# Two layers of a hybrid diffusion backbone: the buffers of the later stages shifted within 512 bytes

## The chip, the core and the metric

The kernel runs on one core of a Trainium2 chip. The core has a matrix engine (TensorE, "PE" in the profile, with its weight loads listed apart as "PEld"), a vector engine (VectorE, "DVE"), a scalar engine (ScalarE, "ACT"), a general engine (GpSimd, "POOL") and a queue engine (SyncE, "SP") that issues most of the transfers. All of them work on one on-chip memory, SBUF, of 128 partitions; matrix products land in a second one, PSUM, of eight banks. An address of a buffer below means its first byte inside each partition.

The metric is device microseconds of one execution. A time is the median of several executions; beside it stands the range. The profile is of one further execution, with its own time.

## The reference

A stream of 512 latent tokens and 256 context tokens, 1,024 wide, passes through two layers. Each sub-layer is norm, modulation, mixer, norm, gate, residual. In outline, with the shapes that matter:

```python
for layer in range(2):
    hl, hc = modulate(rmsnorm(xl), ...), modulate(rmsnorm(xc), ...)
    if layer == 0:
        p = h @ w_in                       # 1024 x 2944: gating MLP + RWKV-7, both directions
        y = concat(spatial_gate(p), rwkv_bidir(p)) @ w_out
    else:
        p = h @ c_w_in                     # 1024 x 2064: mLSTM, 4 heads, both directions
        y = mlstm_out(mlstm_chunk_scan(...)) @ c_w_out
    x = x + gate * rmsnorm(y)
    a, b = split(h @ ffn_up)               # 1024 x 5632
    y = (gelu(depthwise_conv(a)) * b) @ ffn_down      # 2816 x 1024
    x = x + gate * rmsnorm(y)
return xl
```

Layer 1 needs the context tokens only up to the mLSTM's state; its output projection and its ConvFFN run on the 512 latent tokens alone.

## The kernel before

**How a dense product is done.** Everything is kept in float32, and a dense product is made of three products in a reduced format: each operand is split into a rounded part `hi` and a remainder `lo`, and `hi*hi + hi*lo + lo*hi` is accumulated in one PSUM bank. Each contraction step of 128 rows is therefore three matmuls. Such a matmul has a stationary operand of 128 x 128 values (512 bytes in each partition, read by the weight load) and a moving operand of 128 x 512 (latent tokens, or 512 output columns; 2,048 bytes) or 128 x 256 (context tokens). There are two forms:

- `proj_pass` (lines 259 to 270), for `w_in`, `c_in`, the gates and both `ffn_up`: the weight slice is stationary, the transposed tokens `hT` are moving. A pass is 8 contraction steps, 24 matmuls. Names in the profile: `pl_...` for the latent tokens (128x512), `pc_...` for the context (128x256).
- `down` (lines 1033 to 1057), for `w_out`, `c_out` and both `ffn_down`: the tokens are stationary (`a`, `ah`/`al`, or `hhi`/`hlo`), the weight row of 1,024 columns is moving, in halves of 512. Names: `oo` and `of`.

**The stages, in order of time.** Input projections of layer 0 with the preparation of the RWKV scan (to about 380 us of the profiled span), the scan (to 626), `w_out` (to 699), `ffn_up` of layer 0 (to 1075), `ffn_down` of layer 0 (to about 1272), gates, input projections and the mLSTM of layer 1 (to about 1549), `c_out` (to 1584, then the norm), `ffn_up` of layer 1 (1597 to 1843), `ffn_down` of layer 1 (to 1966), the last norm and store.

**What sets the order.** Each engine works through its own list in the order in which the program was written, with generators woven together by hand in the RWKV and mLSTM stages. An instruction waits on semaphores for its operands and for the buffer that it overwrites. In `ffn_up` of layer 0 a filler (`ada_sums`, lines 185 to 205) is woven under the products: five steps for each of the 22 units, all on DVE and POOL.

**Where the buffers lie.** Pools are allocated as two stacks, one from the low end of SBUF upwards, one (`side="right"`) from the high end downwards. A pool begins where the pool under it ends. Tiles inside the pools used by the dense products are multiples of 512 bytes, and the slices that a matmul reads begin at multiples of 512 bytes in them, so all operands of one pool share one offset within 512 bytes. In the built program these are:

| dense product | stationary operand, offset within 512 | moving operand, offset within 512 | matmuls of 128x512 | of 128x256 |
|---|---|---|---|---|
| `w_in` (layer 0 inputs) | weights, right stack: 480 | `hT`, right stack: 480 | 552 | 552 |
| `w_out` | `a`, right stack: 480 | `wo`, left stack: 352 | 288 | 0 |
| `ffn_up`, layer 0 | weights, left stack: 352 | `hT`, right stack: 480 | 1,056 | 1,056 |
| `ffn_down`, layer 0 | `hhi`, `hlo`, left stack, above `fpar`: 224 | weights, left stack: 352 | 792 | 0 |
| gates and `c_in`, layer 1 | weights, left stack: 352 | `hT`, right stack: 480 | 408 | 216 |
| `c_out` | `ah`, `al`, right stack: 480 | `wo`, left stack: 352 | 192 | 0 |
| `ffn_up`, layer 1 | weights, left stack: 352 | `hT`, right stack: 480 | 1,056 | 0 |
| `ffn_down`, layer 1 | `hhi`, `hlo`, left stack: 224 | weights, left stack: 352 | 528 | 0 |

So the input projections of layer 0 have both operands at one offset; in every other dense product they are 128 bytes apart (one way or the other). `fpar`, the table of convolution weights in `ffn`, has 220 values of 4 bytes, 880 bytes, and takes 896 in its pool; the pool `fs`, which holds `hhi` and `hlo`, begins after it.

Of the kernel before, what the change touches and what calls it, by code (L numbers as in the profile page):

```python
# [8 lines left out]
F32 = mybir.dt.float32  # L9
# [5 lines left out]
P = 128  # L15
# [36 lines left out]
PF = _Cols()  # L52
# [17 lines left out]
def build(tc, *args, **kw):  # L70
    with ExitStack() as ctx:
        _build(ctx, tc, *args, **kw)


def _build(ctx, tc, xall, par, cst, ada_0, ada_w, ada_t, w_in, w_out, ffn_up, ffn_down, lora, wsT, a_bs, c_in, c_gate, c_out, mneg, parf, parm, out):
# [983 lines left out]
    def ffn(l, xt, hT, ctx_too, after, final=None, beneath=None):  # L1059

        with ExitStack() as fx:
            hidp = fx.enter_context(tc.tile_pool(name=f"fhid{l}", bufs=1))
            hid = [hidp.tile([P, NH, w], F32, tag=f"hid{g}", name=f"hid{l}{g}") for g, w in ((0, TL), (1, TC))[:2 if ctx_too else 1]]
            fpar = hidp.tile([P, PF.n], F32, name=f"fpar{l}")
            nc.scalar.dma_start(fpar, parf[l])
            sp = fx.enter_context(tc.tile_pool(name=f"fs{l}", bufs=1))
            fill = beneath(sp) if beneath else None
# [71 lines left out]


    strm.sub, strm.hi, strm.lo = nc.vector, 3, 3
    xp = ctx.enter_context(tc.tile_pool(name="x", bufs=1))
    H = {tg: ctx.enter_context(tc.tile_pool(name=f"H{tg}", bufs=1, side="right")) for tg in ("lat", "ctx")}
    xcx = ExitStack()
# [56 lines left out]
    def beneath(pool):  # L1201
# [6 lines left out]
        return ada_sums(rows, place)  # L1208

    ffn(0, xt, hT, True, to_layer1, None, beneath)  # L1210


    xcx.close()
    hT = hT1
    with ExitStack() as ox:
# [280 lines left out]
        with tc.tile_pool(name="op1", bufs=1) as op2:  # L1496
# [9 lines left out]
            hT = h_tiles(H, "h1f", False)  # L1506
            norm_T(1, 1, xt, hT, op2, lambda i: op2.tile([P, D], F32, tag="xin", name=f"xs1{i}", bufs=4), 2, 4, 0, "02461357")
    ffn(1, xt, hT, False, None, out)


# [98 lines left out]
```

## Time and profile before

| | |
|---|---|
| median of 3 executions | 1970.32 us (1968.26 to 1972.65) |
| the profiled execution, its own time | 1975.72 us |
| its span, first to last instruction | 1973.8 us |
| granted TensorE clock, mean over the span | 0.965 |
| PE busy | 1854.0 us, 94% of the span, 12,411 matmuls |
| weight loads busy | 1508.3 us, 76% |
| DVE busy | 1334.4 us, 68% |
| ACT, POOL busy | 800.1 us, 306.9 us |
| moved by DMA | 227.77 MB, mean 115 GB/s |

How to read it. A matmul's row gives its start and a length; the ends are modelled, and matmuls overlap in the array, so that a stream of them has a length of about 0.39 us each and still begins a new one every 0.23 us. What counts for time is the distance from one start to the next. It can be read from the rows in order of time, or from a window in which PE is busy throughout: the window's length over the number of matmuls in it. A window's number in "(x...)" takes in the matmuls that had begun before it and were not over (at 0.39 us of length and 0.23 us of distance, 1.7 of them on the mean). Windows are counted in microseconds from the span's first instruction. Records are to 0.01 us in the rows in order of time.

### The profile page before, as it was taken

The numbers are of one execution on the slowest core, as the hardware profiler recorded it, in microseconds if no ns is written. First come the engines' busy times: TensorE is split into PE (matmuls) and PEld (weight loads), VectorE is DVE, ScalarE is ACT, GpSimd is POOL, SyncE is SP. The second block draws the span as 40 slices with busy tenths as digits, with TensorE's granted clock in tenths as the row PEclk, the third lists the DMA queues.
The fourth block names the chain that finished last, engine by engine and source line by source line (L and its number), as shares of the span: only waits on it lengthen the run. The fifth ranks groups of instructions, "written<-read, shape, count | busy, mean of one in ns | idle before, by whom it ended". The sixth has DMA issues, their size and how long they took to land.

```text
span 1973.8 us, 31872 instructions
## 1 busy us (share of the span) xinstructions
PE 1854.0 (94%) x12411; PEld 1508.3 (76%) x12411; DVE 1334.4 (68%) x2669; ACT 800.1 (41%) x1429; POOL 306.9 (16%) x429
## 2 busy tenths in 40 slices
PE   6998789698898999999999998999999989999998
PEld 4777677587666888888888886778888768888886
DVE  4379675757345589999994337667777688777534
ACT  4364645534335442222222226475554353323222
POOL 2222222311000222223330002100110020000001
PEclk9999889788899999999999999999999999999999
DMA  7133121643764524444432224431111312222222
GB/s 292 54 123 123 57 103 55 182 123 83 204 184 138 182 99 160 150 160 165 161 134 76 97 96 160 151 92 44 33 43 44 139 56 96 96 96 96 88 94 86
DMA packets 102887, 227.77 MB, mean 115 GB/s; under 512 B 28224, under 2 KB 44048, under 8 KB 99664
## 3 DMA queue, kind: packets, MB, share of 16 engines
q1 hardware_dynamic: 100976, 222.26, 33.4%
q10 hardware_dynamic: 1760, 3.47, 0.5%
q8 instruction: 98, 1.61, 0.3%
q14 instruction: 53, 0.43, 0.1%
HBM read 199.31 MB, written 26.39 MB: 114 GB/s over the span
## 4 chain that ended last, share of the span: by engine, by line
PE 58%; DVE 2%; POOL 1%; ACT 1%; issue 1%; DMA 0%; DVEq 0%; SPq 0%; ACTq 0%; POOLq 0%
PE of L1044 5%; PE of L1043 5%; PE of L1045 5%; PE pl_fb L268 4%; PE pl_fb L266 4%; PE pl_fb L267 4%; PE pl_fa L267 4%; PE pl_fa L268 4%; PE pl_fa L266 4%; PE pd L1453 1%; PE pe L1430 1%; PE kv L1386 1%; PE pc_fa L267 1%; PE pc_fa L266 1%; PE pc_fb L266 1%; PE pc_fb L268 1%
## 5 line engine op out<-in xcount | busy, mean ns | idle before, releaser
L1091 DVE SCALAR_TENSOR_TENSOR cv<-pl_fa,fpar,cv 128x441 f32<-128x441 f32 (+2 forms) x352 | 243.1, 691 | 16.5 <-ACT cv L1080 11.3
L1045 PE MATMUL of<-hi_fd,hlo 128*128 128x512 f32 x440 | 173.4, 396 | 3.0 <-DVE hlo L1115 3.0
L1044 PE MATMUL of<-lo_fd,hhi 128*128 128x512 f32 x440 | 174.6, 397 | 1.4 <-DVE lo_fd L125 1.4
L1043 PE MATMUL of<-hi_fd,hhi 128*128 128x512 f32 x440 | 173.7, 397 | 0.0
L201 DVE SCALAR_TENSOR_TENSOR aj<-am,srb 128x512 f32<-128x512 f32 x224 | 163.3, 729 | 10.0 <-DMA am<-in_ada_t_dram 5.6
L1115 DVE TENSOR_TENSOR hlo<-hid,hhi 128x512 fp32r<-128x512 f32 (+1 forms) x66 | 39.2, 601 | 133.9 <-ACT hhi L1114 133.7
L1114 ACT ACTIVATE hhi<-hid 128x512 fp32r<-128x512 f32 (+1 forms) x66 | 36.7, 559 | 177.2 <-PE of L1044 173.5
L1045 PEld LDWEIGHTS of<-hi_fd,hlo 128*128 128x128 f32 x440 | 83.2, 189 | 22.6 <-DVE hlo L1115 3.4
L1044 PEld LDWEIGHTS of<-lo_fd,hhi 128*128 128x128 f32 x440 | 83.3, 189 | 21.5 <-DVE lo_fd L125 2.3
L125 DVE TENSOR_TENSOR lo_fd<-raw_fd,hi_fd 128x1024 fp32r<-128x1024 f32 x66 | 80.8, 1224 | 26.0 <-ACT hi_fd L124 25.8
L1043 PEld LDWEIGHTS of<-hi_fd,hhi 128*128 128x128 f32 x440 | 83.1, 189 | 19.8 <-ACT hi_fd L124 0.5
L222 POOL TENSOR_SCALAR rstd_p_f<-sq_f,sq_f 128x1 f32<-128x1 f32 x10 | 6.9, 689 | 569.6 <-ACT jk_f L1022 569.6
L124 ACT ACTIVATE hi_fd<-raw_fd 128x1024 fp32r<-128x1024 f32 x66 | 69.2, 1049 | 28.7 <-DMA raw_fd<-in_ffn_down_dram 12.2
L124 ACT ACTIVATE hi_fa<-raw_fa 128x1024 fp32r<-128x1024 f32 x44 | 46.4, 1054 | 79.0 <-PE pl_fb L267 64.4
L124 ACT ACTIVATE hi_fb<-raw_fb 128x1024 fp32r<-128x1024 f32 x44 | 46.7, 1061 | 69.6 <-PE pc_fa L267 38.5
L125 POOL TENSOR_TENSOR lo_fb<-raw_fb,hi_fb 128x1024 fp32r<-128x1024 f32 x22 | 59.4, 2699 | 88.8 <-ACT hi_fb L124 88.8
L125 POOL TENSOR_TENSOR lo_win<-raw_win,hi_win 128x1024 fp32r<-128x1024 f32 x23 | 57.5, 2503 | 90.9 <-ACT hi_win L124 90.0
L1093 ACT ACTIVATE cv<-cv 128x512 f32<-128x512 f32 x44 | 27.8, 632 | 106.7 <-DVE cv L1091 106.7
L267 PE MATMUL pl_fa<-h1f_latlo,hi_fa 128*128 128x512 f32 x176 | 69.6, 396 | 0.0
L266 PE MATMUL pl_fb<-h0f_lathi,hi_fb 128*128 128x512 f32 x176 | 69.6, 396 | 0.0
L268 PE MATMUL pl_fa<-h0f_lathi,lo_fa 128*128 128x512 f32 x176 | 69.6, 395 | 0.0
L267 PE MATMUL pl_fb<-h0f_latlo,hi_fb 128*128 128x512 f32 x176 | 69.5, 395 | 0.0
(695 smaller groups left out, 5507.4 us busy)
## 6 DMA issues: line engine op xcount, KB each, us to landing
raw_fd<-in_ffn_down_dram SPq DMA_DIRECT2D x66, 512.0 KB, 3.2
am<-in_ada_t_dram SPq DMA_DIRECT2D x112, 256.0 KB, 3.0
raw_fa<-in_ffn_up_dram SPq DMA_DIRECT2D x44, 512.0 KB, 3.3
raw_fb<-in_ffn_up_dram SPq DMA_DIRECT2D x44, 512.0 KB, 3.2
raw_win<-in_w_in_dram SPq DMA_DIRECT2D x23, 512.0 KB, 3.3
ada<-in_ada_dram SPq DMA_DIRECT2D x8, 1024.0 KB, 8.9
ada<-in_ada_w_dram SPq DMA_DIRECT2D x8, 1024.0 KB, 8.0
raw_cin<-in_c_in_dram SPq DMA_DIRECT2D x16, 512.0 KB, 3.4
```

What stands on the lines that cost most here:

```text
L124: nc.scalar.activation(hi[:, c], raw[:, c], AF.Copy)
L125: strm.sub.tensor_tensor(lo[:, c], raw[:, c], hi[:, c].bitcast(F32), ALU.subtract)
L201: V.scalar_tensor_tensor(place(f"aj{i}{h}{cnd}", "junk"), raw, 1.0, sb[cnd * 2 + h], ALU.mult, ALU.mult, accum_out=acc[:, cnd, h:h + 1])
L266: mm(p, wh[:, kt, :], hh[:, kt], start=(kt == 0), stop=False)
L267: mm(p, wh[:, kt, :], hl[:, kt], start=False, stop=False)
L268: mm(p, wl[:, kt, :], hh[:, kt], start=False, stop=(kt == KT - 1))
L1043: mm(o[i][hf], hi, w[0][:, c], start=f, stop=False)
L1044: mm(o[i][hf], hi, w[1][:, c], start=False, stop=False)
L1045: mm(o[i][hf], lo, w[0][:, c], start=False, stop=e)
L1091: V.scalar_tensor_tensor(dv, src[:, r0 + dy:r1 + dy, c0 + dx:c1 + dx], fw(ky * 3 + kx), dv, ALU.mult, ALU.add)
L1114: A.activation(hi, hid[cnd][:, k], AF.Copy)
L1115: V.tensor_tensor(lo, hid[cnd][:, k], hi.bitcast(F32), ALU.subtract)
```

## The change

Two edits, neither of which touches a computation. A tile of 32 values (128 bytes) named `gap`, which nothing writes or reads, is put on the left stack ahead of the pool `x`. And `fpar` is allocated with 256 values (1,024 bytes) in place of 220; its first 220 are used as before.

```diff
@@ ffn @@
             hidp = fx.enter_context(tc.tile_pool(name=f"fhid{l}", bufs=1))
             hid = [hidp.tile([P, NH, w], F32, ...) for g, w in ((0, TL), (1, TC))[:2 if ctx_too else 1]]
-            fpar = hidp.tile([P, PF.n], F32, name=f"fpar{l}")
+            fpar = hidp.tile([P, 256], F32, name=f"fpar{l}")[:, :PF.n]
             nc.scalar.dma_start(fpar, parf[l])
             sp = fx.enter_context(tc.tile_pool(name=f"fs{l}", bufs=1))
@@ after layer 0's scan @@
     strm.sub, strm.hi, strm.lo = nc.vector, 3, 3
+
+    ctx.enter_context(tc.tile_pool(name="gap", bufs=1)).tile([P, 32], F32, name="gap")
     xp = ctx.enter_context(tc.tile_pool(name="x", bufs=1))
```

In the built program every engine has the same instructions in the same order with the same waits as before; the line numbers after the second edit are two higher. What differs is addresses on the left stack. The pools from `x` upwards (`x`, `xc`, the weight pools `strm` and `strmr`, `wo`, `op0`, `op1`, `wk1` and the others) begin 128 bytes later, at an offset of 480 within 512 where they had 352. The pools `fs0` and `fs1` begin 256 bytes later, at 480 where they had 224. The right stack and everything before `w_out` stay where they were. With that, both operands of every dense product in the table above lie at offset 480. Operands that were not part of a dense product move along: the transposes of the norms and of the mLSTM output (160 in all) now have their two operands 160 or 256 bytes apart where it was 288 or 384; the state products of the mLSTM (`pd`, `pe`) keep their distances, since both operands lie in the same moved pools.

## Prediction

> **What bounds the kernel now.** I read the page first (busy shares, the chain that ended last), then the busy time of each engine by stage, then the rows of single matmuls.
>
> ```profile
> PE 1854.0 (94%) x12411; PEld 1508.3 (76%) x12411; DVE 1334.4 (68%) x2669; ACT 800.1 (41%) x1429; POOL 306.9 (16%) x429
> ...
> PE 58%; DVE 2%; POOL 1%; ACT 1%; issue 1%; DMA 0%; DVEq 0%; SPq 0%; ACTq 0%; POOLq 0%
> ```
>
> PE is busy nearly throughout and carries the chain; no other engine has more than 2% of it. The stages, by windows (columns: length, then busy time and count for PE, weight loads, DVE, ACT, POOL, then PE clock, DMA share, GB/s):
>
> ```profile
> 626.00:699.00 73.00, 70.82 (x320) 57.23 (x320) 44.30 (x74) 38.40 (x77) 13.80 (x19) 1.00 0.52 178
> 699.00:1075.00 376.00, 373.97 (x2130) 325.43 (x2129) 341.71 (x770) 104.09 (x153) 100.68 (x139) 1.00 0.41 142
> 1075.00:1175.00 100.00, 100.00 (x435) 80.76 (x434) 35.25 (x43) 27.96 (x35) 0.00 (x0) 1.00 0.28 98
> 1175.00:1285.00 110.00, 100.68 (x432) 79.47 (x430) 70.30 (x104) 58.42 (x109) 19.30 (x24) 0.95 0.43 151
> 1340.00:1504.00 164.00, 162.72 (x907) 136.04 (x906) 123.03 (x334) 82.52 (x177) 15.01 (x38) 1.00 0.16 46
> 1504.00:1597.00 93.00, 83.23 (x417) 66.10 (x416) 62.57 (x145) 39.25 (x89) 16.39 (x30) 0.96 0.24 85
> 1597.00:1843.00 246.00, 246.00 (x1059) 198.98 (x1058) 192.41 (x256) 81.25 (x98) 0.00 (x0) 1.00 0.26 93
> 1843.00:1966.00 123.00, 122.87 (x529) 99.28 (x527) 46.06 (x53) 36.47 (x54) 3.90 (x6) 1.00 0.24 83
> ```
>
> In both `ffn_up`, both `ffn_down` and `w_out` PE has no idle time to speak of at full clock, so there the time is the number of matmuls times the distance between their starts. The nearest other engine is DVE in `ffn_up` of layer 0, 341.71 of 376 us.
>
> **The price of one matmul, at two placements.** The kernel before has both: `w_in` with its operands at one offset, the rest 128 bytes apart. First the rest, in windows that are all dense matmuls of 128x512 (`ffn_up` of layer 1, `ffn_down` of layer 1 and of layer 0, `w_out`). The first two rows have all engines' columns, the others PE alone; the first is the pass of `w_in` that comes after:
>
> ```profile
> 79.05:84.51 5.46, 5.46 (x26) 4.51 (x25) 2.58 (x1) 1.33 (x2) 2.39 (x1) 1.00 0.13 41
> 1600.00:1840.00 240.00, 240.00 (x1035) 194.53 (x1034) 186.65 (x246) 79.39 (x94) 0.00 (x0) 1.00 0.26 93
> ...
> 1845.00:1965.00 120.00, 120.00 (x518) 1.00 0.24 84
> 1080.00:1195.00 115.00, 115.00 (x496) 1.00 0.28 98
> 632.00:672.00 40.00, 40.00 (x174) 1.00 0.68 230
> ```
>
> With 1.7 taken off each count for those begun before: 240/1033.3 = 232.3 ns, 120/516.3 = 232.4, 115/494.3 = 232.7, 40/172.3 = 232.2. One price, whichever operand lies on which stack, and whether DMA runs at 84 or 230 GB/s and DVE is 37% or 78% busy (46.06 of 123, 186.65 of 240). Now the pass of `w_in`, at the same clock of 1.00, in rows of time (start, length), 24 latent matmuls and then the context ones:
>
> ```profile
> 79.05 0.40 PE L266 MATMUL pl_kT<-h_lathi,hi_win 128*128 128x512 f32 x1
> ...
> 80.43 0.39 PE L266 MATMUL pl_kT<-h_lathi,hi_win 128*128 128x512 f32 x1
> ...
> 83.83 0.39 PE L266 MATMUL pl_kT<-h_lathi,hi_win 128*128 128x512 f32 x1
> ...
> 84.51 0.28 PE L266 MATMUL pc_kT<-h_ctxhi,hi_win 128*128 128x256 f32 x1
> ...
> 87.27 0.28 PE L268 MATMUL pc_kT<-h_ctxhi,lo_win 128*128 128x256 f32 x1
> ```
>
> From 80.43 to 83.83 lie 15 distances: 3.40/15 = 226.7 ns. The first six of the pass are longer, 1.38/6 = 230.0; the pass with its step into the next is 5.46/24 = 227.5. In the pass the distance between the two operands' addresses changes by 1,536 bytes at each contraction step, and the price stays 226.7: only the place within 512 bytes is the same throughout. The context matmuls, 24 starts: (87.27 - 84.51)/23 = 120.0. Their like in `ffn_up` of layer 0, 128 bytes apart:
>
> ```profile
> 903.62 0.28 PE L266 MATMUL pc_fb<-h0f_ctxhi,hi_fb 128*128 128x256 f32 x1
> ...
> 906.35 0.28 PE L268 MATMUL pc_fb<-h0f_ctxhi,lo_fb 128*128 128x256 f32 x1
> ...
> 906.92 0.40 PE L268 MATMUL pl_fa<-h0f_lathi,lo_fa 128*128 128x512 f32 x1
> 907.17 0.40 PE L266 MATMUL pl_fa<-h0f_lathi,hi_fa 128*128 128x512 f32 x1
> ...
> 908.55 0.40 PE L266 MATMUL pl_fa<-h0f_lathi,hi_fa 128*128 128x512 f32 x1
> 908.79 0.40 PE L267 MATMUL pl_fa<-h0f_latlo,hi_fa 128*128 128x512 f32 x1
> ```
>
> 2.73/23 = 118.7. So one offset makes the wide matmul 5.6 ns shorter once it has settled (232.3 - 226.7), 4.8 in passes of 24 between narrow ones (232.3 - 227.5), and the narrow one 1.3 ns longer (the rows' 0.01 us leave about 0.6 on that). The last four rows show how the 128 bytes cost: one long distance (907.17 - 906.92 = 0.25) and the next long one 7 starts later (908.79 - 908.55 = 0.24); the seven from 906.92 to 908.55 are 1.63/7 = 232.9. The slowness turns up in a cycle, as if two reads drift past each other; at one offset they lock, and stay at the short distance.
>
> [...]
>
> **The change part by part.** Nothing is added to any engine's list and no wait changes; the cost of the two edits themselves is nothing. The 4,320 wide matmuls outside `w_in` and the 1,272 narrow ones get the other price. The unmoved `w_in` does not change. By stage:
>
> - `ffn_up` of layer 0, 1,056 wide in passes of 24 and 1,056 narrow: 1,056 x 4.8 = 5.1 us, less 1,056 x 1.3 = 1.4, so 3.7. PE would need some 372 us of the stage, DVE 342: PE stays the bound, with 30 us before DVE takes over.
> - `ffn_down` of layer 0, 792 wide: 792 x 5.6 = 4.4. In its end (1175 to 1285) PE idles 9.3 of 110 us round the norms and gates, so I take 4.1.
> - `ffn_up` of layer 1, unbroken: 1,056 x 5.6 = 5.9. `ffn_down` of layer 1: 528 x 5.6 = 3.0.
> - `w_out`: 288 x 5.6 = 1.6. `c_out`: 192 x 5.6 = 1.1, of which I take 0.8, since PE idles in a tenth of that window (83.23 of 93).
> - Gates and `c_in`: 408 x 4.8 = 2.0 at most, less 216 x 1.3 = 0.3. They are woven among the mLSTM's chain, where the wide matmuls come late rather than slow:
>
> ```profile
> L266 PE MATMUL pl_xm<-h_lathi,hi_cin 128*128 128x512 f32 x64 | 27.1, 423 | 0.0
> ...
> L267 PE MATMUL pl_fa<-h1f_latlo,hi_fa 128*128 128x512 f32 x176 | 69.6, 396 | 0.0
> ...
> L253 PE MATMUL nT<-cst_s,xs_lat 128*128 128x128 f32 x32 | 4.2, 275 | 1.7 <-ACT hf L255 1.7
> ...
> L1476 PE MATMUL hT<-cst_s,hs 128*128 128x128 f32 x32 | 6.4, 283 | 1.9 <-DVE hs L1471 1.9
> ```
>
> A mean of 423 ns there against 396 in the dense stage shows matmuls that waited; a shorter one ahead of a wait gives nothing. Between 0 and 1.7 I take 0.7.
> - The 160 transposes that now have another distance: the two last rows, at 288 and 384 bytes, differ by 8 ns, so 160 x 8 = 1.3 us either way at the most; I take 0.
> - ACT, DVE and POOL read and write at the new places too. ACT's rounding of a weight tile is the one row that exists at both offsets, 480 in `w_in` and 352 in `ffn_up`:
>
> ```profile
> L124 ACT ACTIVATE hi_fb<-raw_fb 128x1024 fp32r<-128x1024 f32 x44 | 46.7, 1061 | 69.6 <-PE pc_fa L267 38.5 <-PE pl_fa L267 26.4 <-DMA raw_fb<-in_ffn_up_dram 4.7
> ...
> L124 ACT ACTIVATE hi_win<-raw_win 128x1024 fp32r<-128x1024 f32 x23 | 24.1, 1057 | 21.1 <-PE pc_u L267 6.6 <-issue 5.3 <-PE pc_kT L267 2.7
> ```
>
> 1061 and 1057: nothing. A DVE row at both is missing; PE hides it in every dense stage until DVE gets 9% slower (372/342).
>
> Sum: 3.7 + 4.1 + 5.9 + 3.0 + 1.6 + 0.8 + 0.7 = 19.8 us. Against the profiled execution's own 1975.72 that is 1955.9, a ratio of 0.990; on the median of the runs, 1970.32, it gives 1950.6. **I predict 1951 us.** Bounds of the unknown: if the dense streams never settle and stay at the 230.0 of a pass's first six, the gain is 4,320 x 2.3 = 9.9, less 1,272 x 1.3 = 1.7, so 8.2 and 1962; if every wide matmul settles and counts and the narrow ones lose nothing, 4,320 x 5.6 = 24.2 and 1946.
>
> **The rivals.**
>
> *The offset is not the cause.* The `w_in` stage could be quicker for another reason, its pools (all on the right stack) or its neighbours' work, and the changed kernel keeps 232.3: 1970. For it: `w_in` is the only stage with equal offsets, so stage and offset cannot be told apart in this trace. [...] Against it: the slow price is the same in four stages of different load, operand order and buffers, and the quick one holds while DVE and POOL are busy for nearly half of the pass (2.58 and 2.39 of 5.46 us).
>
> *Another engine takes the gain.* In `ffn_up` of layer 0 DVE, with its filler, is close behind, and round the mLSTM and `c_out` the chain decides: these three give nothing, 19.8 - 3.7 - 0.7 - 0.8 = 14.6, hence 1956. Against it: 30 us of room.
>
> *The streams lock at the long distance (slower).* If equal offsets stop the drift, they stop it at whatever phase the stream has; in `w_in` each pass reached the short one, but `down` enters from other work and has the weights as its moving operand. A stream held at the long distance costs 0.24 instead of 0.2323, 8 ns more. All 4,320 there: 34.6 us, hence 2005. It decides the sign once the held share is over 5.6/(5.6 + 8) = 41% of the matmuls. Against it: six distances into the pass quoted the short one is reached, and a stream that can leave the long phase there can do so elsewhere.
>
> **How the numbers follow.** The forecast 0.80, another engine taking part of it 0.07, offset not the cause 0.08, locking at the long distance 0.05. Faster by over 0.2% (3.9 us, about what a measurement of this kernel can tell from no change): 0.80 + 0.07 = 0.87; same 0.08; slower 0.05. The range takes the two bounds, 1946 and 1962, and 1 us below for the scatter of the runs (1968.26 to 1972.65): 1945 to 1962; it holds the second rival's 1956 too and leaves out the other two, 0.13, and a little of the first case.
>
> **What would show it.** In the changed kernel's windows of `ffn_up` and `ffn_down` of layer 1, PE busy throughout with a distance near 227 ns: about 1,060 matmuls in 240 us instead of 1,035, and those stages ending 5.9 and 3.0 us sooner. The narrow matmuls of `ffn_up`, layer 0, at 120. `w_in` unchanged. If the distance is 232 in all stages, the first rival holds; if it is 227 and the time stays, PE must show idle time in `ffn_up` of layer 0 ended by DVE; a distance of 240 in `of` or `oo` would be the third. The forecast is wrong if the four dense stages together do not give at least 10 us.

## The result, and the profile after

The changed kernel takes 1954.29 us (median of 4, 1950.92 to 1954.95); the kernel before, run beside it, 1971.49 (4, 1968.26 to 1974.81). The ratio is 0.9913, with a 95% interval of 0.9896 to 0.9929: faster by 0.9%, 17.2 us by the medians. The profiled execution took 1954.95 us, its span 1952.9, at the same mean clock of 0.965.

First the page of the changed kernel, the busy shares and the chain that ended last:

```profile
PE 1831.6 (94%) x12411; PEld 1505.0 (77%) x12411; DVE 1332.2 (68%) x2669; ACT 800.6 (41%) x1429; POOL 307.2 (16%) x429
...
PE 57%; DVE 2%; ACT 2%; POOL 2%; issue 1%; DMA 0%; POOLq 0%; DVEq 0%; ACTq 0%
```

PE still bounds the kernel, with as many matmuls, but is busy 22.4 us less; DVE, ACT, POOL and the weight loads stay within 4 us of what they were. The same stages as shown of before, by windows of the changed kernel (same columns):

```profile
624.00:695.00 71.00, 69.03 (x318) 56.88 (x319) 43.83 (x74) 37.80 (x76) 13.84 (x19) 1.00 0.53 182
695.00:1067.00 372.00, 369.93 (x2129) 325.90 (x2128) 341.92 (x770) 104.17 (x155) 100.91 (x139) 1.00 0.42 144
1067.00:1167.00 100.00, 100.00 (x446) 82.44 (x445) 35.92 (x44) 29.27 (x37) 0.00 (x0) 1.00 0.29 101
1167.00:1273.00 106.00, 96.86 (x423) 77.00 (x421) 69.23 (x104) 57.57 (x108) 19.49 (x24) 0.97 0.45 154
1328.00:1492.00 164.00, 162.48 (x907) 136.06 (x905) 122.87 (x334) 82.73 (x178) 15.35 (x38) 1.00 0.16 46
1492.00:1584.00 92.00, 81.77 (x413) 65.45 (x413) 62.13 (x144) 38.52 (x89) 15.46 (x29) 0.96 0.25 86
1584.00:1824.00 240.00, 240.00 (x1061) 198.19 (x1060) 190.81 (x255) 81.52 (x97) 0.00 (x0) 1.00 0.27 95
1824.00:1945.00 121.00, 120.43 (x532) 99.31 (x530) 47.35 (x55) 36.69 (x55) 3.53 (x6) 1.00 0.25 85
```

The same work now stands in shorter windows. Read the third row against its like before: in 100 us of `ffn_down`, layer 0, 446 matmuls where there were 435, at the same clock. And the seventh: 1,061 in 240 us of `ffn_up`, layer 1. The clean windows of wide matmuls give the price of one, as before with 1.7 taken off each count (columns: PE alone; `ffn_up` of layer 1, `ffn_down` of layer 1 and of layer 0, `w_out`):

```profile
1586.00:1820.00 234.00, 234.00 (x1032) 1.00 0.27 95
1826.00:1942.00 116.00, 116.00 (x513) 1.00 0.25 86
1070.00:1180.00 110.00, 110.00 (x487) 1.00 0.29 101
632.00:667.00 35.00, 35.00 (x156) 1.00 0.68 230
```

234/1030.3 = 227.1 ns, then 226.9, 226.7 and 226.8, where all four were at 232.2 to 232.7.

**Where the time came from.** The part ahead of `w_out` is untouched, and yet not equally long in two executions. The start of `w_out` is the first start in these rows (one line's matmuls, with the first and the last start in us), of the kernel before, of the changed kernel, and of a second profile of the changed kernel:

```profile
L1043 PE MATMUL oo<-hi_wo,a_lathi x64: 390/393/503, 627.2 to 672.4; 128*128 128x512 f32 x64
```

```profile
L1043 PE MATMUL oo<-hi_wo,a_lathi x64: 389/389/499, 624.8 to 668.9; 128*128 128x512 f32 x64
```

```profile
L1043 PE MATMUL oo<-hi_wo,a_lathi x64: 389/389/504, 618.5 to 662.7; 128*128 128x512 f32 x64
```

So 2.4 of the 20.9 us between the two first spans (1973.8 and 1952.9) are of a part in which nothing was changed; in all profiles of this study its length varies from 617 to 627 us. What the change did is read from `w_out` on: 1346.6 us before, 1328.1 after (18.5 less), 1329.5 in the second profile (17.1 less). By stage, each from its first matmul to the first one of the next:

| stage, us | before | after | second profile of after | predicted gain | measured gain |
|---|---|---|---|---|---|
| `w_out` | 72.2 | 70.8 | 71.0 | 1.6 | 1.4, 1.2 |
| `ffn_up`, layer 0 | 375.9 | 371.7 | 371.7 | 3.7 | 4.2, 4.2 |
| `ffn_down`, layer 0 | 198.0 | 194.6 | 195.2 | 4.1 | 3.4, 2.8 |
| gates | 11.7 | 10.8 | 10.7 | } 0.7 | 0.9, 1.0 |
| `c_in`, mLSTM | 219.2 | 219.1 | 219.0 | } | 0.1, 0.2 |
| `c_out` | 93.0 | 92.6 | 94.0 | 0.8 | 0.4, -1.0 |
| `ffn_up`, layer 1 | 245.9 | 240.0 | 239.5 | 5.9 | 5.9, 6.4 |
| `ffn_down`, layer 1 | 122.5 | 119.5 | 119.5 | 3.0 | 3.0, 3.0 |
| last norm and store | 8.4 | 8.9 | 8.9 | 0 | -0.5, -0.5 |
| sum | 1346.6 | 1328.1 | 1329.5 | 19.8 | 18.5, 17.1 |

### The profile page after: what moved, and what is told of

The parts are those of the page before. It is cut to its first block, busy times and chain, and to the rows that moved or that the text cites. A ratio compares the mean times of both kernels' runs of the same rounds, so it can differ in the third digit from the quotient of the medians.

```text
span 1952.9 us, 31872 instructions
## 1 busy us (share of the span) xinstructions
PE 1831.6 (94%) x12411; PEld 1505.0 (77%) x12411; DVE 1332.2 (68%) x2669; ACT 800.6 (41%) x1429; POOL 307.2 (16%) x429
## 4 chain that ended last, share of the span: by engine, by line
PE 57%; DVE 2%; ACT 2%; POOL 2%; issue 1%; DMA 0%; POOLq 0%; DVEq 0%; ACTq 0%
PE of L1044 5%; PE of L1045 5%; PE of L1043 5%; PE pl_fb L267 4%; PE pl_fb L268 4%; PE pl_fb L266 4%; PE pl_fa L267 4%; PE pl_fa L266 4%; PE pl_fa L268 4%; PE pd L1455 1%; PE pe L1432 1%; PE pc_fb L268 1%; PE pc_fa L268 1%; PE pc_fb L267 1%; PE pc_fa L267 1%; PE pc_fb L266 1%
## 5 line engine op out<-in xcount | busy, mean ns | idle before, releaser
L266 PE MATMUL pl_fa<-h0f_lathi,hi_fa 128*128 128x512 f32 x176 | 69.0, 392 | 0.0
L267 PE MATMUL pl_fa<-h0f_latlo,hi_fa 128*128 128x512 f32 x176 | 68.9, 391 | 0.0
```

The source lines that it names most:

```text
L266: mm(p, wh[:, kt, :], hh[:, kt], start=(kt == 0), stop=False)
L267: mm(p, wh[:, kt, :], hl[:, kt], start=False, stop=False)
```

## The experiments

Theory: what counts is how far the moving operand lies from the stationary one within some power of two of bytes, and equal places are the best. Rivals: the place of either operand by itself; the stage and what runs beside it; the dense streams merely becoming shorter the nearer the two lie (a graded cost). In all experiments the instructions, their order and their waits are those of the kernel before; only addresses differ, and the arithmetic is whole. Edits are given against the changed kernel. "Distance" is the moving operand's address less the stationary one's, within 512 bytes; before it was 128 or, in `w_out` and `c_out`, 384.

### Thirteen other distances: four kernels

Three numbers set the distances: the size of `gap` moves the weights of `ffn_up` and the rest of the left stack, the size of `fpar` the tokens of `ffn_down` of each layer, and a further empty tile ahead of the pool of `wo` the weights of `w_out` and `c_out`.

```diff
-    ...tile_pool(name="gap", bufs=1)).tile([P, 32], F32, name="gap")
+    ...tile_pool(name="gap", bufs=1)).tile([P, G], F32, name="gap")
-            fpar = hidp.tile([P, 256], F32, name=f"fpar{l}")[:, :PF.n]
+            fpar = hidp.tile([P, (F0, F1)[l]], F32, name=f"fpar{l}")[:, :PF.n]
+        ox.enter_context(tc.tile_pool(name="gapw", bufs=1)).tile([P, W], F32, name="gapw")
```

With G, F0, F1, W of 16, 248, 232, 56, the distances are 64 in `ffn_up`, 32 and 96 in `ffn_down` of layers 0 and 1, 160 in `w_out`:

> Only the sizes of the two gap-like allocations differ from the changed kernel, and one more gap stands ahead of the w_out pools. Distance within 512 bytes, moving operand minus stationary one: ffn_up (both layers) and c_in 64, ffn_down of layer 0 32, ffn_down of layer 1 96, w_out 160, c_out 448. Equality theory (only one and the same place locks, every other place drifts): 232.3 ns from start to start of the wide matmuls in all of them, and the time of the kernel before, about 1971 us. Graded theory (the price grows with the distance): ffn_down of layer 0 at 32 bytes near 227 to 228 ns, ffn_up at 64 near 229, ffn_down of layer 1 at 96 near 231, w_out at 232 or more, time near 1962. Third possibility, a place that is better than equality: some stage below 226.7 ns.

With 96, 336, 328, 8: 256, 192, 224, 288.

> As the first of these, with distances: ffn_up and c_in 256, ffn_down of layer 0 192, ffn_down of layer 1 224, w_out 288, c_out 256. Equality theory: 232.3 ns everywhere, about 1971 us. Graded theory: these are the farthest places, so they cost more than the 232.3 seen at 128, for instance 235 ns, and the time is above 1975. A place better than equality: below 226.7 ns in one of the stages.

With 48, 304, 296, 88: 448, 320, 352, 416.

> As the first of these, with distances: ffn_up and c_in 448 (64 bytes the other way round), ffn_down of layer 0 320, ffn_down of layer 1 352, w_out 416, c_out 64. Equality theory: 232.3 ns everywhere, about 1971 us. Graded theory: ffn_up as at 64, near 229; w_out near 231; ffn_down 233 to 235; time near 1967. If only the sign decides (the weight load behind or ahead of the stream), ffn_up at 448 differs from ffn_up at 64.

With 40, 264, 272, 8: 480, 480, 448, 64.

> As the first of these, with distances: ffn_up and c_in 480 (32 bytes the other way round), ffn_down of layer 0 480, ffn_down of layer 1 448, w_out 64, c_out 32. Equality theory: 232.3 ns everywhere, about 1971 us. Graded theory: ffn_up and ffn_down of layer 0 at 227 to 228, ffn_down of layer 1 and w_out near 229, time near 1957. The same distance in two stages (480 in ffn_up and ffn_down, 448 in ffn_down here and ffn_up in the run before, 64 in w_out here and ffn_up in the first) gives the same price if the distance alone decides.

Times of one execution each, beside 1969.86 of the kernel before: 1967.82, 1958.66, 1965.79 and 1968.58. Only the second, with `ffn_up` at 256, comes near the changed kernel. The clean windows of the first (PE alone; `ffn_up` of layer 1, `ffn_down` of layer 0, `w_out`):

```profile
1600.00:1830.00 230.00, 230.00 (x1006) 1.00 0.29 97
1080.00:1190.00 110.00, 110.00 (x473) 1.00 0.29 96
...
640.00:676.00 36.00, 36.00 (x155) 1.00 0.65 215
```

Of the second (`ffn_up` 1, `ffn_down` 0, `ffn_down` 1, `w_out`):

```profile
1600.00:1820.00 220.00, 220.00 (x973) 1.00 0.29 98
1068.00:1180.00 112.00, 112.00 (x482) 1.00 0.29 99
1830.00:1945.00 115.00, 115.00 (x494) 1.00 0.23 79
628.00:664.00 36.00, 36.00 (x156) 1.00 0.67 223
```

Of the third, in the same order:

```profile
1600.00:1830.00 230.00, 230.00 (x987) 1.00 0.28 94
1080.00:1190.00 110.00, 110.00 (x482) 1.00 0.30 101
1840.00:1950.00 110.00, 110.00 (x473) 1.00 0.24 82
636.00:672.00 36.00, 36.00 (x155) 1.00 0.62 201
```

And of the fourth:

```profile
1600.00:1830.00 230.00, 230.00 (x988) 1.00 0.29 96
1075.00:1185.00 110.00, 110.00 (x473) 1.00 0.29 96
1840.00:1955.00 115.00, 115.00 (x494) 1.00 0.23 79
634.00:670.00 36.00, 36.00 (x159) 1.00 0.60 193
```

The first row of the second kernel is the finding: 220/971.3 = 226.5 ns with the operands 256 bytes apart, as good as equal places. The price of a wide matmul at each distance, as the mean of the distances from start to start in the stage (the windows above give the same to 0.6 ns); a distance stands beside the one 256 bytes further:

| distance | price, ns | distance | price, ns |
|---|---|---|---|
| 0 | 226.7 | 256 | 226.8 |
| 32 | 233.3 | 288 | 233.3 |
| 64 | 228.8 to 229.0 | 320 | 229.0 |
| 96 | 233.4 | 352 | 233.3 |
| 128 | 232.4 | 384 | 232.4 |
| 160 | 234.3 | 416 | 234.3 |
| 192 | 233.4 | 448 | 233.3 to 233.4 |
| 224 | 233.3 | 480 | 233.2 to 233.4 |

The two columns agree in all eight rows, to 0.2 ns: over these sixteen distances the price repeats every 256 bytes. It is not graded: 32 bytes away is worse (233.3 ns) than 64 (229.0) or 128 (232.4). So neither of the two theories that the expectations set against each other holds: the first wanted 232.3 at every distance but 0, the second a price that grows with the distance. A distance that stands in two stages or with the operands' roles exchanged has one price (64 in `ffn_up` and `w_out`, 448 in `ffn_up` and `ffn_down`). And nothing was found below 226.7.

### The second edit alone

```diff
-    ctx.enter_context(tc.tile_pool(name="gap", bufs=1)).tile([P, 32], F32, name="gap")
```

Now `ffn_down` has both operands at 352, and `ffn_up`, `w_out` and `c_out` are as before.

> The larger fpar alone, no gap. Both operands of ffn_down then lie at 352 (equal, but not at the place 480 of the other equal ones); every other dense product stays 128 bytes apart. If only the distance counts: ffn_down of both layers at 226.7 ns, ffn_up at 232.3, w_out at 232.3; the gain is that of the two ffn_down stages, some 3.3 + 3.0 = 6.3 us, ratio about 0.9968. If the place 480 itself counts: ffn_down stays at 232 and the ratio is 1.000.

Measured 1967.11 us, ratio 0.9974 (0.9959 to 0.9989). The windows (`ffn_down` of layer 1 and of layer 0, `ffn_up` of layer 1):

```profile
1845.00:1960.00 115.00, 115.00 (x509) 1.00 0.25 86
1080.00:1190.00 110.00, 110.00 (x487) 1.00 0.31 103
1600.00:1835.00 235.00, 235.00 (x1013) 1.00 0.29 95
```

115/507.3 and 110/485.3 are 226.7 each, 235/1011.3 is 232.4. In `ffn_down` the weights have not moved at all, and the tokens lie at 352 where the changed kernel has them at 480: neither place matters, the distance does. From `w_out` on it takes 1342.2 us, 4.4 less than before; the two `ffn_down` stages gave 2.1 and 3.0 of the 3.3 and 3.0 that were expected. The gates went from 11.7 to 10.8 us here too, though their operands are 128 bytes apart as before. With 256 bytes between them, in the second of the four kernels, they took 11.7. So that gain is not of their distance.

### The first edit alone

```diff
-            fpar = hidp.tile([P, 256], F32, name=f"fpar{l}")[:, :PF.n]
+            fpar = hidp.tile([P, 220], F32, name=f"fpar{l}")[:, :PF.n]
```

> The gap alone, fpar as it was. ffn_down stays 128 bytes apart (352 and 480), everything else is equal. If the parts add: ffn_down at 232.3 ns, ffn_up and w_out at 226.7 to 227.9; the gain is 1.3 (w_out) + 4.1 (ffn_up 0) + 0.9 (gates) + 0.4 (c_out) + 5.8 (ffn_up 1) = 12.5 us by the stages of the changed kernel, ratio about 0.9937. If they do not add (a stage takes the gain of another): well off that.

Measured 1957.11 us, ratio 0.9927 (0.9908 to 0.9947). `ffn_up` of layer 1, then `ffn_down` of layers 1 and 0:

```profile
1590.00:1820.00 230.00, 230.00 (x1016) 1.00 0.29 99
1826.00:1942.00 116.00, 116.00 (x501) 1.00 0.24 82
1064.00:1176.00 112.00, 112.00 (x483) 1.00 0.30 100
```

226.8, 232.3 and 232.7. From `w_out` on 1334.0 us, 12.6 less. The two edits add: 4.4 + 12.6 = 17.0, against 18.5 and 17.1 for both together.

### The good stage made bad

Eight values (32 bytes) of empty tile on the right stack ahead of `hT` of layer 0 put the operands of `w_in` 32 bytes apart (480 in the terms of the table), in the one stage that had them equal in both kernels.

```diff
+        hx.enter_context(tc.tile_pool(name="gapr", bufs=1, side="right")).tile([P, 8], F32, name="gapr")
```

> The changed kernel with a gap of 32 bytes on the right stack between the weights and the tokens of w_in, the only stage that was equal before: distance 480 there. If the offset is the cause and not the stage: the settled price of the wide matmuls of w_in goes from 226.7 to about 233.3 ns and of the narrow ones from 119.7 to about 118.6, as in ffn_up at distance 480. If the stage is the cause: 226.7 stays. The time hardly shows it, at most 552 x 6.6 = 3.6 us, since the RWKV preparation paces part of that stage.

One execution, 1956.46 us (1972.36 for the kernel before beside it). The pass shown in the prediction, in rows of time:

```profile
78.68 0.40 PE L266 MATMUL pl_kT<-h_lathi,hi_win 128*128 128x512 f32 x1
...
84.05 0.40 PE L268 MATMUL pl_kT<-h_lathi,lo_win 128*128 128x512 f32 x1
84.28 0.28 PE L266 MATMUL pc_kT<-h_ctxhi,hi_win 128*128 128x256 f32 x1
```

5.60/24 = 233.3 ns where it was 227.5: the stage has no virtue of its own. By the starts, the narrow passes of the stage take 118.0 to 118.7 ns a matmul where nearly all had 119.7, as expected. What this costs in all can't be read from one execution, since `w_out` began at 624.2 us, inside the 617 to 627 of the other kernels.

### How exact equality must be

In `ffn_down` of layer 1 the tokens' tiles are 640 values wide and the slice begins 1 value in for the first 11 steps, 4 values in for the other 11: 4 bytes and 16 bytes off equal (508 and 496 in the terms of the table, since it is the stationary operand that moves).

```diff
+                    n, s = (640, 1 if k < 11 else 4) if l else (512, 0)
-                    hi = sp.tile([P, 512], F32R, tag="hhi", ...)[:, :w]
+                    hi = sp.tile([P, n], F32R, tag="hhi", ...)[:, s:s + w]
```

(`lo` likewise.)

> The changed kernel with the token operand of ffn_down of layer 1 moved inside its tile, by 4 bytes in the first 11 contraction steps and by 16 bytes in the others. If the places must be equal to the byte: 233 ns in both halves. If a memory line of some 32 bytes or more is what counts: 226.7 at 4 bytes and perhaps at 16. If the cost comes from the relative phase of two streams of 4 bytes a step: 4 bytes is one step, and shifts the price by little.

One execution, 1958.31 us. The first half of the stage and the second:

```profile
1826.00:1885.00 59.00, 59.00 (x255) 1.00 0.28 92
1888.00:1946.00 58.00, 58.00 (x251) 1.00 0.21 73
```

59/253.3 = 232.9 and 58/249.3 = 232.7; by the starts 232.4 and 233.3. One value off is as bad as 128 bytes off.

### The context operand elsewhere

In the third of the four kernels above `ffn_up` of layer 0 had its operands 448 bytes apart, and there the narrow matmuls took 113.5 ns, less than at any other distance. Here the wide ones stay at 0 and the narrow ones get 448: 16 empty values between the latent and the context tokens on the right stack (and 48 further on, so that the mLSTM's output comes to lie 256 bytes from the weights of `c_out`). The 96 matmuls of `w_out` with context tokens get 64.

```diff
+    ctx.enter_context(tc.tile_pool(name="gapc", bufs=1, side="right")).tile([P, 16], F32, name="gapc")
+            ox.enter_context(tc.tile_pool(name="gapa", bufs=1, side="right")).tile([P, 48], F32, name="gapa")
```

> The changed kernel with the context pool moved 64 bytes down on the right stack (and 192 more under it, for c_out): the narrow matmuls of ffn_up and c_in have distance 448, the wide ones stay at 0; 96 wide ones of w_out go to 64. If the price of a matmul is set by its own distance: narrow ones 113.5 ns as in the run with distance 448, wide ones 227.9, so 1,056 x 6.1 = 6.4 us less in ffn_up of layer 0, w_out 96 x 2.3 = 0.2 us more, and some 0.5 us less in c_in, where half or less counts: a further 6 to 7 us under the changed kernel, ratio to the kernel before about 0.988. If the price comes from the pair (what one matmul's weight load meets is the stream of the one before), the passes that change from wide to narrow lose a little, but 22 of 24 in each pass still gain. If DVE, which would then have 342 of some 361 us, becomes the bound: less than 6 us, with PE waits for DVE in ffn_up of layer 0.

Measured 1953.18 us (1948.44 to 1956.46), ratio 0.9905 (0.9886 to 0.9924). The changed kernel, run again beside it:

> The changed kernel unchanged, for comparison on the same chip: ratio 0.990 to 0.992.

gave 1952.07 us (1948.51 to 1962.04), ratio 0.9910 (0.9886 to 0.9933). The totals don't tell the two apart. The stage does: `ffn_up` of layer 0 took 368.6 us in place of 371.7, half of what was expected. Its rows, first of the changed kernel, then of this one (start, length; from the first wide matmul of a pass to the first one after the context):

```profile
892.22 0.40 PE L266 MATMUL pl_fb<-h0f_lathi,hi_fb 128*128 128x512 f32 x1
...
893.61 0.39 PE L266 MATMUL pl_fb<-h0f_lathi,hi_fb 128*128 128x512 f32 x1
...
897.69 0.28 PE L266 MATMUL pc_fb<-h0f_ctxhi,hi_fb 128*128 128x256 f32 x1
...
900.56 0.40 PE L266 MATMUL pl_fa<-h0f_lathi,hi_fa 128*128 128x512 f32 x1
```

```profile
900.60 0.39 PE L266 MATMUL pl_fa<-h0f_lathi,hi_fa 128*128 128x512 f32 x1
...
906.04 0.28 PE L266 MATMUL pc_fa<-h0f_ctxhi,hi_fa 128*128 128x256 f32 x1
...
908.86 0.39 PE L266 MATMUL pl_fb<-h0f_lathi,hi_fb 128*128 128x512 f32 x1
```

In the changed kernel a wide pass takes (897.69 - 892.22)/24 = 227.9 ns a matmul, its first six distances 1.39/6 = 231.7; here (906.04 - 900.60)/24 = 226.7, so the slow start is gone. The narrow pass takes 2.87/24 = 119.6 there and 2.82/24 = 117.5 here, not 113.5; over the whole stage, by the starts, 119.7 and 117.8. These two make up the gain: 1,056 x 1.2 + 1,056 x 1.9 = 3.3 for the 3.1 measured. PE's distances of more than 0.5 us in the stage add up to 3.25 us there and 3.30 here, so DVE did not take the rest. A narrow matmul at distance 448 has had two prices, 113.5 and 117.8, and something beside its own distance decides between them. The wide passes in between differ (at 448 there, at 0 here), and so do the places themselves; whether it is one of these is open.

## Why the prediction was right, and where it was off

**The main step, the price by the distance.** Right. The prediction took 226.7 ns for a settled wide stream, from one pass of `w_in`; the four stages came to 226.7 to 227.1. The terms that are nothing but this price held: `ffn_up` of layer 1 5.9 and 6.4 for 5.9, `ffn_down` of layer 1 3.0 and 3.0 for 3.0, `w_out` 1.4 and 1.2 for 1.6. That it is the distance, and not the stage or a place, was argued there and is shown by the second edit alone and by the good stage made bad.

**"Only the place within 512 bytes."** Too narrow a reading of one stage. The distance in `w_in` changes by 1,536 bytes at a time, which is a multiple of 512 and of 256; the runs show 256.

**`ffn_up` of layer 0: 3.7 predicted, 4.2 measured.** The wide term was right: by the starts, the latent passes went from 244.8 to 239.8 us, 5.0 for 5.1 (232.7 and 227.9 ns a matmul). The narrow term was too large: from rows of 0.01 us the prediction took 1.3 ns, and the context passes went from 125.5 to 126.3 us, 0.8 for 1.4. 5.0 - 0.8 = 4.2. PE's idle time in the stage's window stayed at 2 us (2.03 of 376 before, 2.07 of 372 after), so DVE's 341.92 us stayed hidden.

**`ffn_down` of layer 0: 4.1 predicted, 3.4 and 2.8 measured.** The step that was mis-sized is the small allowance for the stage's end. By the starts, the 528 matmuls of the latent tokens went from 122.8 to 119.9 us, 2.9, which is their price. The 264 of the context tokens went from 73.55 to 73.09, and to 73.63 in the second profile: hardly a gain, where 264 x 5.6 = 1.5 was at stake. With the second edit alone, equal places too, it is 74.32; with the first alone, at the old distance, 73.28. Two things besides the matmuls set the length of this part. One is PE's waits for DVE and ACT: 3.0, 1.7 and 1.4 us before, 3.1, 2.0 and 0.8 after, 3.1, 1.8 and 0.4 in the second profile, so they did not grow in all. The other is the granted clock behind the first of these waits. Six microseconds at the same place of the part, before, after, and in the second profile of after (PE alone, then clock, DMA share and GB/s):

```profile
1208.90:1214.90 6.00, 6.00 (x19) 0.72 0.91 313
```

```profile
1198.10:1204.10 6.00, 5.83 (x25) 1.00 0.95 299
```

```profile
1191.90:1197.90 6.00, 5.77 (x14) 0.51 0.86 314
```

Seven, none and twelve matmuls begin there 426 to 427 ns after the one before. The two last differ without any change to the kernel. How much of the missing 1.5 falls to the clock and how much to the waits is open.

**Gates and `c_in`: 0.7 predicted, 1.0 and 1.2.** Right in size by luck. The gates' 0.9 is not of their distance (the second edit alone has it, the kernel with 256 bytes has not). It goes with the granted clock again, behind a wait of 2.6 us between two starts; six microseconds of the gates before and after, in which eleven and seven matmuls begin 426 to 427 ns after the one before:

```profile
1276.00:1282.00 6.00, 5.87 (x15) 0.54 0.24 87
```

```profile
1264.80:1270.80 6.00, 5.90 (x21) 0.72 0.28 87
```

The same stretch has 0.72 with the second edit alone and 0.54 in the kernel with 256 bytes. `c_in` with the mLSTM, where the term was meant to lie, gave 0.1 and 0.2, in a stage that takes from 217.2 to 220.5 us in the profiles of this study: the matmuls that "came late rather than slow" gave nothing that shows.

**`c_out`: 0.8 predicted, 0.4 and -1.0.** The term itself was about right: PE's long wait for the norm begins 79.8 us into the stage before, 79.2 in both profiles after, 0.6 sooner. What differs is the end of the stage, the last 3 us ahead of `ffn_up`, in the first and in the second profile of after:

```profile
1581.50:1584.50 3.00, 3.00 (x22) 0.78 0.00 0
```

```profile
1577.10:1580.10 3.00, 3.00 (x16) 0.50 0.00 0
```

The last 13 of the transposes there begin 109 ns apart in the one and 213 in the other, 13 x 0.104 = 1.4 us.

**The tail: 0 predicted, -0.5.** It is 0.5 longer in all five profiles with equal places in `ffn_down` of layer 1 (8.9, against 8.3 to 8.6 in the others). POOL's last two small instructions wait for ACT, and DVE's last work waits for them. Here is the first of the two before, and then after, with the row of DVE ahead of it:

```profile
1966.90 0.30 POOL L222 TENSOR_SCALAR rstd_p_f<-sq_f,sq_f 128x1 f32<-128x1 f32 x1 [1.20 <-ACT jk_f L1022]
```

```profile
1945.30 1.28 DVE L1029 TENSOR_TENSOR xb<-pt_f,xb 128x512 f32<-128x512 f32 x2
...
1945.68 0.98 POOL L222 TENSOR_SCALAR rstd_p_f<-sq_f,sq_f 128x1 f32<-128x1 f32 x1 [1.80 <-ACT jk_f L1022]
```

ACT's last step, behind work of DVE, comes 0.2 us later after the last matmul (0.86 for 0.64); then POOL's instruction falls inside DVE's and takes 0.98 in place of 0.30 (the one behind it 0.56 in place of 0.88). DVE's new addresses have no part in it that shows: its instructions there take 0.68 to 0.69 and 0.74 to 0.75 us each in all profiles. What makes POOL's first instruction longer there, no run shows.

**The sum.** 19.8 against 18.5 and 17.1 by the stages, and 17.2 by the medians. The dense streams alone gave what was priced; 1.3 to 2.7 us are missing in `ffn_down`'s context part, at the end of `c_out` and in the tail, places where PE waits, or where the granted clock is not the same in two executions. The forecast of 1951 us missed by 3.3: 1.2 of it is the kernel before, 1971.49 beside this run against the 1970.32 that the forecast started from, and 2.6 the sum, less 0.5 by which the forecast was rounded up.

**The rivals.** That the offset is not the cause is out by the stage's own reversal. That another engine takes the gain is out for `ffn_up`, layer 0, but true on a small scale for the mLSTM; for the context part of `ffn_down` it is open. Locking at the long distance is out for equal places: no stream of them settled anywhere but at 226.7. But prices above the 232.4 of the kernel before do exist, 234.3 at 160 bytes, so that a change of offsets can also lose.

**The picture of two reads.** With the same stream in the same place, moving what the weight load reads by 128 bytes changes the spacing from 232.4 to 226.7 ns (`ffn_down` of layer 1, the second edit alone). How the one read comes to act on the other no run here shows; "as if two reads drift past each other" remains a picture. It fits the starts: in `ffn_up` of layer 1 the distances of the kernel before go round every seven starts, from 228 up to 241 ns, and in the changed kernel 1,023 of 1,055 are 226 or 227.

## What to carry to other kernels

Where matmuls with a weight load each run back to back at full clock, and PE sets the time, look at the addresses of both operands in the built program: a distance that is a multiple of 256 bytes between them was worth 2.5% of a stream of 128x512 here (and cost 0.6% of one of 128x256), costs a few hundred bytes of memory and no instruction, and a single value off loses it (232.4 ns in place of 226.7). Price it with windows in which PE is busy throughout, and count it only for those matmuls: ahead of a wait it was given back here (`c_in` with the mLSTM gained 0.1 and 0.2 us). When an untouched part of the program varies by 10 us between executions, compare stages, not spans; and ahead of reading a microsecond in a stage where PE waits, look at the granted clock of the same stretch in both.

## What was not expected

- The period of 256 bytes: 226.8 ns at 256, and eight pairs of distances that agree to 0.2 ns.
- No slope toward equal places: 232.4 ns at 4 bytes (508), 233.3 at 16 (496) and at 32, 229.0 at 64, 234.3 at 160.
- Narrow matmuls follow another curve: 119.7 ns at 0 and at 256, 118.9 at 128, 117.8 at 64, 118.6 at 480, and at 448 113.5 in one kernel and 117.8 in another.
- The slow first six matmuls of a wide pass depend on the narrow pass ahead: 231.7 ns after narrow ones at distance 0, 226.7 after narrow ones at 448.
- Two profiles of one kernel differ by 1.4 us in `c_out` (92.6 and 94.0), with a granted clock of 0.78 and 0.50 over the 3 us ahead of `ffn_up` of layer 1.
